# A transformer block on one core: the squares of x1 and the first down weights queued on VectorE and ScalarE behind the first product's second sum

## The chip, the core and the metric

The kernel runs on one core of a Trainium2 chip. A core has five engines that work side by side, each through its own queue in order: TensorE (PE; its weight loads are listed as PEld), VectorE (DVE), ScalarE (ACT), GpSimd (POOL) and SyncE (SP), which here issues all DMAs. The metric is the time of one execution in microseconds on the device. The kernel before takes 1398.54 us, the median of three runs from 1398.4 to 1398.91.

## The reference, cut to what matters

One layer of a hybrid block on 1024 tokens of width 1024, all in float32: a norm, a projection, three mixers (attention, a state-space scan, a gated recurrence), an output projection, and then the gated feed-forward part with 2816 inner columns that the change touches:

```
x = x + concatenate([att, ssd, lru]) @ w_out          # this is x1 below
h = rmsnorm(x, norm_ffn)                              # x1 * rsqrt(mean(x1^2)) * g
x = x + (silu(h @ w_gate) * (h @ w_up)) @ w_down
return rmsnorm(x, norm_final)
```

## The kernel before, in words

Everything is kept transposed, channels on the partitions and tokens along the row. Products in float32 are made from two halves: a high half (ACT copies the data in TensorE's rounded format) and a low half (DVE subtracts the high one from the source). Three matmuls, high by high, high by low and low by high, then stand for one. The helper `split` (L78 for ACT's copy, L69 for DVE's subtraction) does this, and `operand` makes such a pair in a tile of tag h.

`att_proj` ends the output projection. Each of its 16 units of 12 matmuls gives half a row block of x1; `finish` adds the residual (DVE, L75), scales it with the norm's weights (ACT), stores x1 to memory (`x1d`) and writes the pieces that the feed-forward products need, as split pairs, into tiles A and h.

The feed-forward products use a scheme with seven block products for eight. A product (`product(j, m, ...)`, j for one of 11 pairs of weight blocks, m = 0 for gate and 1 for up) loads a pair of weight blocks, wst and whi (l11, l12, l21, l22 are their halves), and makes four combinations of them in two tiles of tag t, s12 and s34. Seven chains of 12 matmuls follow (L955; the text calls them by the index of the pieces that they read): chains 0, 5, 6 and 4 add up in one bank x, and ACT copies its state after each of them (c11, c12, c21, c22); chains 1, 3 and 2 go to banks of their own (mm) and DVE and POOL add these to the copies. Chain 6 may start only when c12 has been copied out of x, chain 4 only after c21. For c21, POOL subtracts c21 from c12 (L69), and DVE then adds chain 3's bank to c21 (`add(V, c21, y2, c21)`, L1004). The four combinations are DVE's in the first product (0, 0) and POOL's in all others. In this text the first, second and third product are (0, 0), (0, 1) and (1, 0).

`squares` (L904) follows the first product in the program. It loads the eight row blocks of x1 again (L908; the first into ssum2, the other seven into tiles of tag g, which has two places), ACT squares each, and DVE adds seven of them to ssum2. `down_weights(0)` (L1013) loads a pair of w_down, makes four combinations of it on DVE in two tiles of tag t, and stores them. ssum2 is read by `rnorm_small` (L1072), 16 small matmuls behind the second product's chain 6; `factor` spreads its result over a tile r2 behind the third product's chain 5, and the gating of the first two pairs (`gated`, `to_down`) needs r2.

The order of the queues is set by a planner. It goes by its own clock through the program; among the instructions of an engine whose inputs are there and whose tiles have a place, it takes the one that stands first in the program. The engine then works in that order, whether or not the chip agrees with the planner's clock. A tag has a fixed number of places (wst 2, whi 2, t 4, g 2, e 4, h 16). `tc.issue_after(ins)` adds, for each instruction traced in its block that is on the same engine as `ins`, an edge that puts it behind `ins` on that engine's queue; instructions of other engines get none. `marks` lists matmuls: marks[1] is the last of the first product's chain 6.

Of the kernel before, what the change touches and what calls it, by code (L numbers as in the profile page):

```python
# [38 lines left out]
def tile_hybrid_block(ctx: ExitStack, tc: tile.TileContext, xT, w_in, w_dt, w_out, w_gu, w_dn, lru_g, prm,  # L39
                      c_ident, c_tri, c_last, c_alibi, outT, probe=None, stop=None):  # L40
    nc = tc.nc
    V, A, G, T = nc.vector, nc.scalar, nc.gpsimd, nc.tensor
# [16 lines left out]
    def bank():  # L59
        return psm.tile([P, H2], F32, name="mm", tag="mm")  # L60
# [7 lines left out]
    def sub(eng, out, a, b):  # L68
        return eng.tensor_tensor(out=out, in0=a, in1=b, op=ALU.subtract)  # L69
# [4 lines left out]
    def add(eng, out, a, b):  # L74
        return eng.tensor_tensor(out=out, in0=a, in1=b, op=ALU.add)  # L75

    def act(out, in_, func, **kw):
        return A.activation(out=out, in_=in_, func=func, **kw)  # L78
# [55 lines left out]
    def rnorm_small(sums, n, eps, pn_pool, tag="p1"):  # L134

        nb = sums[0].shape[-1] // P
        pn = pn_pool.tile([P, 8], F32, name=tag, tag=tag)[:, :nb]
        for tb in range(nb):
            for j, s in enumerate(sums):
                pn_last[0] = T.matmul(pn[:, tb:tb + 1], lhsT=s[:, tb * P:tb * P + P], rhs=ones[:, 0:1],  # L140
                                      start=(j == 0), stop=(j == len(sums) - 1))
        rn = sm.tile([P, 8], F32, name="rn", tag="rn")[:, :nb]
        rn_last[0] = rsqrt_small(rn, pn, n, eps)
        return rn
# [37 lines left out]
    with tc.tile_pool(name="np", bufs=2) as npool:  # L182
# [18 lines left out]
        last_mm = [None]  # L201
# [636 lines left out]
    def duo(pool, tag, dt=F32, bufs=None):  # L838
        return pool.tile([P, 2, H2], dt, name=tag, tag=tag, bufs=bufs)

    def combine_l(engs, s12, s34, l11, l12, l21, l22):
        e = iter(engs * 4)
        add(next(e), s12[:, 0], l21, l22)
        sub(next(e), s12[:, 1], s12[:, 0], l11)
        sub(next(e), s34[:, 0], l11, l21)
        sub(next(e), s34[:, 1], l12, s12[:, 1])
# [57 lines left out]
    def squares():  # L904

        for n in range(8):
            sq = ssum2 if n == 0 else slot(fp, "g", bufs=2)
            dma(out=sq, in_=x1d[n])  # L908
            act(sq, sq, AF.Square)
            if n:  # L910
                add(V, ssum2, ssum2, sq)

    NP = NFF // 2
    last_mm, last_hi = [None], [None]

    def operand(src):
        o = duo(hp, "h", F32R)
        act(o[:, 0], src, AF.Copy)
        sub(V, o[:, 1], src, f(o[:, 0]))
        return o  # L920

    def pair_loads(src, j):
        a, b = slot(wp, "wst", bufs=2), slot(wp, "whi", bufs=2)
        dma(out=a, in_=src[j])
        dma(out=b, in_=src[j + NP])
        return a, b
# [24 lines left out]
    def chain(ps, w, i, start, stop, ks=range(4)):  # L951
        for k in ks:
            ws = slice(k * P, k * P + P)
            for n, (wi, ai) in enumerate(((0, 0), (0, 1), (1, 0))):
                last_mm[0] = T.matmul(ps, lhsT=w[:, wi, ws], rhs=ops[k][i][:, ai], start=(start and k == 0 and n == 0),  # L955
                                      stop=(stop and k == 3 and n == 2), skip_group_check=not start)

    def product(j, m, ca, cb, hook=None):

        a, b = pair_loads(w_gu[m], j) if j or m else first[:2]  # L960
        l11, l12, l21, l22 = a[:, :H2], a[:, H2:], b[:, :H2], b[:, H2:]
        s12, s34 = duo(fp, "t", bufs=4), duo(fp, "t", bufs=4)
        if j or m:
            combine_l((G,), s12, s34, l11, l12, l21, l22)
        else:
            add(V, s12[:, 0], l21, l22)
            sub(V, s12[:, 1], s12[:, 0], l11)
            with tc.issue_after(last_put[0].ins):
                sub(V, s34[:, 0], l11, l21)
                sub(V, s34[:, 1], l12, s12[:, 1])  # L970
        x = psx.tile([P, H2], F32, name="x", tag="x")
        c11, c12, c21, c22 = ca[:, :H2], ca[:, H2:], cb[:, :H2], cb[:, H2:]
        if j == 0 and m == 0:

            y, y2, s2 = bank(), bank(), operand(s12[:, 1])
            chain(x, first[2][0], 0, True, True)
            chain(y, first[2][1], 1, True, True)
            for ks in (range(3), range(3, 4)):
                chain(y2, first[2][2], 3, True, True, ks)
                if ks[0] == 0:  # L980
                    act(c11, x, AF.Copy)
                chain(x, s2, 5, False, True, ks)
        else:
            chain(x, operand(l11), 0, True, True)
            y = bank()
            chain(y, operand(l12), 1, True, True)
            y2 = None
        if y2 is None:
            act(c11, x, AF.Copy)
        add(V, c11, y, c11)  # L990
        if y2 is None:
            chain(x, operand(s12[:, 1]), 5, False, True)
        marks.append(last_mm[0])
        if hook:
            hook()
        act(c12, x, AF.Copy)
        if y2 is None:
            y2 = bank()
            chain(y2, operand(l22), 3, True, True)
        chain(x, operand(s34[:, 0]), 6, False, True)  # L1000
        marks.append(last_mm[0])
        last_hi[0] = act(c21, x, AF.Copy)
        sub(G, c12, c12, c21)
        add(V, c21, y2, c21)  # L1004
        y = bank()
        chain(y, operand(s34[:, 1]), 2, True, True)
        chain(x, operand(s12[:, 0]), 4, False, True)
        marks.append(last_mm[0])
        act(c22, x, AF.Copy)
        add(G, c12, c12, c22)  # L1010
        add(V, c12, y, c12)

    def down_weights(j):  # L1013
        a, b = pair_loads(w_dn, j)
        s12, s34 = duo(fp, "t", bufs=4), duo(fp, "t", bufs=4)
        combine_l((V,), s12, s34, a[:, :H2], b[:, :H2], a[:, H2:], b[:, H2:])
        dma(out=wdd[0:2, j].rearrange("s p c -> p s c"), in_=s12)
        dma(out=wdd[2:4, j].rearrange("s p c -> p s c"), in_=s34)

    turn = [0]  # L1020
    marks = []

    def chunks():
        turn[0] += 1
        return [slot(fp, "g", bufs=2) if turn[0] % 3 == 0 else ev() for _ in range(2)]

    def gated(ga, gb):
        for g in (ga, gb):
            mul(V, g, g, r2[0])
            silu = act(g, g, AF.Silu)  # L1030
            mul(G, g, g, r2[0])
        return silu

    def to_down(j, ga, gb, ua, ub):
        mul(V, ga, ga, ua)
        mul(V, gb, gb, ub)
        t12, t34 = duo(wp, "wlo", bufs=2), duo(wp, "wlo", bufs=2)
        combine_r((V,), t12, t34, ga[:, :H2], ga[:, H2:], gb[:, :H2], gb[:, H2:])
        dma(out=sd[0, j], in_=ga[:, :H2])
        dma(out=sd[1:3, j].rearrange("s p c -> p s c"), in_=gb.rearrange("p (s c) -> p s c", s=2))  # L1040
        dma(out=sd[3:5, j].rearrange("s p c -> p s c"), in_=t12)
        dma(out=sd[5:7, j].rearrange("s p c -> p s c"), in_=t34)
# [13 lines left out]
    for j in range(NP):  # L1056
        ga, gb = chunks()
        product(j, 0, ga, gb, factor if j == 1 else None)
        if j == 0:
            with tc.issue_after(marks[1].ins):  # L1060
                squares()
                down_weights(j)
        else:
            silu = gated(ga, gb)
            if j == NP - 1:
                with tc.issue_after(silu.ins):
                    act(eps, ones[:, 0:1], AF.Sqrt)
            down_weights(j)
        ua, ub = chunks()
        product(j, 1, ua, ub)  # L1070
        if j == 0:
            with tc.issue_after(marks[4].ins):  # L1072
                late[0] = rnorm_small([ssum2], 1024.0, 1e-6, psy, tag="mm")
            held0 = ga, gb, ua, ub
        else:
            to_down(j, ga, gb, ua, ub)
# [226 lines left out]
```

## Time and profile before

| | us |
|---|---|
| median of 3 runs | 1398.54 |
| lowest, highest | 1398.4, 1398.91 |
| the profiled execution | 1396.86 |
| its span, first to last instruction | 1395.1 |

Times in the rows are microseconds from the start of the span; "mean ns" and forms are left as the profile prints them. "wst", "t" and so on are tile names with their numbers left out, so t<-whi is an instruction that reads tile whi and writes a tile t. In square brackets stands the engine's idle time before an instruction and what ended it. TensorE's granted clock is given as a share of 2.4 GHz; its other level is 1.2 GHz. SPq is the issue of a DMA, which lands later.

### The profile page before, as it was taken

The numbers are of one execution on the slowest core, as the hardware profiler recorded it, in microseconds if no ns is written. First come the engines' busy times: TensorE is split into PE (matmuls) and PEld (weight loads), VectorE is DVE, ScalarE is ACT, GpSimd is POOL, SyncE is SP. The second block draws the span as 40 slices with busy tenths as digits, with TensorE's granted clock in tenths as the row PEclk, the third lists the DMA queues.
The fourth block names the chain that finished last, engine by engine and source line by source line (L and its number), as shares of the span: only waits on it lengthen the run. The fifth ranks groups of instructions, "written<-read, shape, count | busy, mean of one in ns | idle before, by whom it ended". The sixth has DMA issues, their size and how long they took to land.

```text
span 1395.1 us, 18403 instructions
## 1 busy us (share of the span) xinstructions
PE 1341.3 (96%) x6786; PEld 1123.1 (81%) x6786; DVE 989.4 (71%) x1538; ACT 662.5 (47%) x1076; POOL 366.1 (26%) x265
## 2 busy tenths in 40 slices
PE   7999898999999899999979999999999999999996
PEld 6888588878888688788858878888888888888896
DVE  8667648988254677886797887876777676665655
ACT  5385746555232666765664433343332335543432
POOL 0022103766000000000005566664555642000000
PEclk9999999999999899999989999999999999999998
DMA  5112122332227865430356344444544348866523
GB/s 204 53 46 76 46 77 66 93 126 81 76 103 223 293 211 123 120 91 16 127 176 225 104 154 144 158 151 159 174 168 138 130 167 302 310 196 196 186 87 121
DMA packets 90266, 198.66 MB, mean 142 GB/s; under 512 B 9272, under 2 KB 23992, under 8 KB 90176
## 3 DMA queue, kind: packets, MB, share of 16 engines
q1 hardware_dynamic: 90176, 197.49, 43.0%
q8 instruction: 53, 0.87, 0.3%
q14 instruction: 37, 0.30, 0.1%
HBM read 142.64 MB, written 54.82 MB: 142 GB/s over the span
## 4 chain that ended last, share of the span: by engine, by line
PE 73%; DVE 11%; ACT 5%; DMA 5%; issue 3%; POOL 3%; SPq 0%; DVEq 0%; ACTq 0%; POOLq 0%
PE mm L98 17%; PE x L955 15%; PE mm L955 11%; PE mm L1106 11%; PE x L1106 4%; PE mm L425 2%; PE pt L726 2%; PE p L198 2%; DMA x1d<-e 1%; PE po L743 1%; PE sc L683 1%; PE sc L682 1%; DVE h L69 1%; PE po L745 1%; DMA acb<-acd 1%
## 5 line engine op out<-in xcount | busy, mean ns | idle before, releaser
L98 PE MATMUL mm<-h,whi 128*128 128x512 f32 x1184 | 373.4, 394 | 1.8 <-ACT h L78 1.1
L98 PEld LDWEIGHTS mm<-h,whi 128*128 128x128 f32 x1184 | 220.6, 188 | 46.6 <-ACT h L78 1.8
L98 PE MATMUL mm<-h,wlo 128*128 128x512 f32 x592 | 231.6, 392 | 0.0
L955 PE MATMUL x<-A,h 128*128 128x512 f32 x726 | 185.0, 398 | 4.5 <-ACT e L78 2.4
L955 PEld LDWEIGHTS x<-A,h 128*128 128x128 f32 x726 | 137.4, 190 | 37.4 <-ACT e L78 3.6
L75 POOL TENSOR_TENSOR t<-whi 128x512 f32<-128x512 f32 x21 | 32.7, 1557 | 458.3 <-DVE h L69 384.4
L1106 PE MATMUL mm<-h 128*128 128x512 f32 (+1 forms) x666 | 150.1, 378 | 0.0
L1106 PEld LDWEIGHTS mm<-h 128*128 128x128 f32 x666 | 120.2, 188 | 23.5 <-DVE h L69 0.4
L955 PE MATMUL mm<-A,h 128*128 128x512 f32 x528 | 136.4, 395 | 0.0
L98 PEld LDWEIGHTS mm<-h,wlo 128*128 128x128 f32 x592 | 111.5, 188 | 23.3 <-DVE wlo L69 0.3
L955 PEld LDWEIGHTS mm<-A,h 128*128 128x128 f32 x528 | 99.2, 188 | 23.1
L69 DVE TENSOR_TENSOR h<-t,h 128x512 fp32r<-128x512 f32 x97 | 100.4, 1052 | 20.6 <-ACT h L78 20.5
L78 ACT ACTIVATE e<-x 128x512 f32<-128x512 f32 x60 | 35.8, 596 | 129.1 <-PE x L955 114.1
L69 DVE TENSOR_TENSOR h<-wst,h 128x512 fp32r<-128x512 f32 (+1 forms) x70 | 77.4, 1124 | 24.5 <-ACT h L78 24.5
L955 PE MATMUL x<-h 128*128 128x512 f32 x330 | 92.4, 399 | 0.0
L955 PE MATMUL mm<-h 128*128 128x512 f32 x264 | 75.9, 398 | 8.2 <-ACT h L78 5.5
L78 ACT ACTIVATE whi<-wst 128x1024 fp32r<-128x1024 f32 x44 | 46.4, 1055 | 65.6 <-PE mm L98 52.1
L955 PEld LDWEIGHTS x<-h 128*128 128x128 f32 x330 | 63.4, 192 | 14.8
L78 ACT ACTIVATE h<-wst 128x512 fp32r<-128x512 f32 (+1 forms) x70 | 53.4, 786 | 36.6 <-DMA whi<-sd 11.6
L69 DVE TENSOR_TENSOR h<-whi,h 128x1024 fp32r<-128x1024 f32 (+1 forms) x47 | 53.5, 1138 | 23.9 <-ACT h L78 23.6
L69 DVE TENSOR_TENSOR wlo<-wst,whi 128x1024 fp32r<-128x1024 f32 x44 | 56.7, 1288 | 17.1 <-ACT whi L78 16.9
L955 PEld LDWEIGHTS mm<-h 128*128 128x128 f32 x264 | 49.8, 189 | 20.6 <-ACT h L78 5.9
(281 smaller groups left out, 2618.1 us busy)
## 6 DMA issues: line engine op xcount, KB each, us to landing
wst<-w_in SPq DMA_DIRECT2D x32, 512.0 KB, 3.6
qkl<-qkd SPq DMA_DIRECT2D x48, 256.0 KB, 5.7
wst<-w_gu SPq DMA_DIRECT2D x22, 512.0 KB, 4.4
whi<-w_gu SPq DMA_DIRECT2D x22, 512.0 KB, 5.4
wdd<-t SPq DMA_DIRECT2D x22, 512.0 KB, 4.7
sd<-wlo SPq DMA_DIRECT2D x22, 512.0 KB, 4.7
qkd<-e SPq DMA_DIRECT2D x16, 512.0 KB, 3.4
wst<-sd SPq DMA_DIRECT2D x28, 256.0 KB, 3.5
```

What stands on the lines that cost most here:

```text
L69: return eng.tensor_tensor(out=out, in0=a, in1=b, op=ALU.subtract)
L75: return eng.tensor_tensor(out=out, in0=a, in1=b, op=ALU.add)
L78: return A.activation(out=out, in_=in_, func=func, **kw)
L98: mm = T.matmul(ps, lhsT=w[:, ws], rhs=a[:, sl], start=(k == 0 and n == 0), stop=(k == nk - 1 and n == 2))
L198: last_mm[0] = T.matmul(os[hf], lhsT=w[:, ws], rhs=a[:, hf * H2:hf * H2 + H2], start=(kk == 0 and n == 0), stop=(kk == KD - 1 and n == 2))
L425: T.matmul(o, lhsT=a[k][:, ts], rhs=w, start=(k == 0 and n == 0), stop=(k == KD - 1 and n == 2))
L682: T.matmul(sc[:, :w], lhsT=qs[:, qc], rhs=ks[:, kc], start=True, stop=False)
L683: gate[0] = T.matmul(sc[:, :w], lhsT=qs[:, qc], rhs=kl[:, kc], start=False, stop=True)
L726: T.transpose(pt[:, j, qi * P:qi * P + P], pes[qi][:, kb * P:kb * P + P], ident)
L743: T.matmul(po[0:64, q0:], lhsT=va[:, 0:64], rhs=plo, start=False, stop=False)
L955: last_mm[0] = T.matmul(ps, lhsT=w[:, wi, ws], rhs=ops[k][i][:, ai], start=(start and k == 0 and n == 0), stop=(stop and k == 3 and n == 2 ...
L1106: mm = T.matmul(banks[n][:, cols], lhsT=w[:, 0, ws], rhs=a[:, 1, cols], start=(start and j == 0 and m == 0), stop=(stop and j == NP - 1 an ...
```

## The change

The block around `squares()` and `down_weights(0)` names two other instructions: DVE's add that completes c21 of the first product, and ACT's copy of c21. Both blocks are open at once, so what the two functions have on DVE stands behind the add, and what they have on ACT behind the copy. Their DMAs, on SP, get no edge.

```
-    last_mm, last_hi = [None], [None]
+    last_mm, last_hi, out_dve = [None], [None], [None]
...
         last_hi[0] = act(c21, x, AF.Copy)
         sub(G, c12, c12, c21)
-        add(V, c21, y2, c21)
+        out_dve[0] = add(V, c21, y2, c21)
...
         if j == 0:
-            with tc.issue_after(marks[1].ins):
+            with tc.issue_after(out_dve[0].ins), tc.issue_after(last_hi[0].ins):
                 squares()
                 down_weights(j)
```

## Rows read from the trace of the kernel before

**Rows 1.** The page's first part: busy time, share of the span, instructions.
```profile
PE 1341.3 (96%) x6786; PEld 1123.1 (81%) x6786; DVE 989.4 (71%) x1538; ACT 662.5 (47%) x1076; POOL 366.1 (26%) x265
```

**Rows 2.** Table of stretches: length, busy time (instructions) by engine, PEclk, DMA share, GB/s.
```profile
720.00:730.00 10.00, 1.85 (x4) 1.12 (x4) 7.70 (x12) 6.88 (x10) 0.00 (x0) 0.67 0.64 219
730.00:740.00 10.00, 7.93 (x25) 5.87 (x24) 10.00 (x15) 5.51 (x8) 3.09 (x1) 0.65 0.67 216
740.00:760.00 20.00, 20.00 (x89) 16.22 (x88) 15.63 (x17) 7.47 (x14) 15.64 (x10) 1.00 0.46 157
```

**Rows 3.** Timeline of TensorE: start, length, line, operation, tiles, count [idle time before].
```profile
719.47 0.61 PE L955 MATMUL mm<-h 128*128 128x512 f32 x2
725.55 0.79 PE L955 MATMUL mm<-h 128*128 128x512 f32 x1 [5.47 <-ACT h L78]
729.02 1.22 PE L955 MATMUL mm<-h 128*128 128x512 f32 x2 [2.68 <-DVE h L69]
...
733.17 3.36 PE L955 MATMUL x<-A,h 128*128 128x512 f32 x7 [2.07 <-DVE h L69]
...
737.31 1.54 PE L955 MATMUL mm<-A,h 128*128 128x512 f32 x6
```

**Rows 4.** Timeline of ACT, 716 to 747 us.
```profile
716.54 0.71 ACT L78 ACTIVATE t<-e,pr 128x512 f32<-128x512 f32 x1
721.31 1.06 ACT L78 ACTIVATE g<-g 128x1024 f32<-128x1024 f32 x1 [4.06 <-DMA g<-x1d]
...
744.51 0.63 ACT L78 ACTIVATE h<-t 128x512 fp32r<-128x512 f32 x1 [5.09 <-POOL t L69]
745.05 0.62 ACT L78 ACTIVATE h<-whi 128x512 fp32r<-128x512 f32 x1
...
746.09 0.58 ACT L78 ACTIVATE e<-x 128x512 f32<-128x512 f32 x1
```

**Rows 5.** Timeline of DVE, 700 to 751 us.
```profile
700.31 1.21 DVE L75 TENSOR_TENSOR ssum<-ssum,g 128x1024 f32<-128x1024 f32 x1
...
718.82 1.28 DVE L69 TENSOR_TENSOR t<-t 128x512 f32<-128x512 f32 x2
722.40 1.22 DVE L75 TENSOR_TENSOR ssum<-ssum,g 128x1024 f32<-128x1024 f32 x1 [2.30 <-ACT g L78]
...
730.09 1.21 DVE L75 TENSOR_TENSOR ssum<-ssum,g 128x1024 f32<-128x1024 f32 x1
...
732.43 0.68 DVE L69 TENSOR_TENSOR h<-t,h 128x512 fp32r<-128x512 f32 x1
733.03 0.68 DVE L75 TENSOR_TENSOR t<-wst,whi 128x512 f32<-128x512 f32 x1
...
739.52 1.28 DVE L69 TENSOR_TENSOR h<-wst,h 128x512 fp32r<-128x512 f32 x2
...
750.33 0.68 DVE L75 TENSOR_TENSOR e<-mm,e 128x512 f32<-128x512 f32 x1
```

**Rows 6.** Timeline of POOL, 736 to 770 us.
```profile
736.91 5.06 POOL L75 TENSOR_TENSOR t<-whi 128x512 f32<-128x512 f32 x1 [384.39 <-DVE h L69]
...
743.18 1.30 POOL L69 TENSOR_TENSOR t<-t,wst 128x512 f32<-128x512 f32 x1
...
746.75 1.41 POOL L69 TENSOR_TENSOR e<-e 128x512 f32<-128x512 f32 x1 [0.89 <-ACT e L78]
...
754.95 1.75 POOL L75 TENSOR_TENSOR e<-e 128x512 f32<-128x512 f32 x1
...
767.72 1.29 POOL L69 TENSOR_TENSOR t<-t,wst 128x512 f32<-128x512 f32 x1
```

**Rows 7.** All that line 908 issues: its loads of x1, issue to landing.
```profile
DMA to landing us min/median/max: 3.1/3.4/5.3
```

**Rows 8.** Timeline of TensorE: the statistics, and the next long wait.
```profile
762.28 1.84 PE L140 MATMUL mm<-ones,ssum 128*128 128x1 f32 x16
...
807.63 2.09 PE L955 MATMUL x<-A,h 128*128 128x512 f32 x6 [2.17 <-ACT e L78]
```

More of the change, by code (lines that the diff above doesn't have):

```diff
@@ L913, in tile_hybrid_block @@
     NP = NFF // 2
-    last_mm, last_hi = [None], [None]
+    last_mm, last_hi, out_dve = [None], [None], [None]
     def operand(src):
@@ L1003, in product @@
         sub(G, c12, c12, c21)
-        add(V, c21, y2, c21)
+        out_dve[0] = add(V, c21, y2, c21)
         y = bank()
@@ L1059, in tile_hybrid_block @@
         if j == 0:
-            with tc.issue_after(marks[1].ins):
+            with tc.issue_after(out_dve[0].ins), tc.issue_after(last_hi[0].ins):
                 squares()
```

## The prediction, made before the changed kernel was run

> **What bounds the kernel now.** The page comes first: TensorE is busy for 1341.3 of 1395.1 us [rows 1], so a change is worth what it takes from TensorE's remaining losses. The table of stretches shows the largest of them: from 720 to 740 us the granted clock averages 0.67 and 0.65, a mixture of 2.4 and 1.2 GHz, and 4 + 25 matmuls pass, against 89 in the next 20 us, 0.225 us apart [rows 2]. At that pace 29 matmuls are 6.5 us, so the place loses 13.5 us. TensorE's timeline gives its make-up: the engine runs dry at 720.08 (719.47 + 0.61), waits 5.47, 2.68 and 2.07 us, and goes on at full pace from 737.31 [rows 3]. The waits are 10.2 us; the other 3.3 are matmuls at half clock behind them. It waits for pieces of the first product's chains 3 and 5, each split into two halves, the high one by ACT, the low one by DVE.
>
> ACT's timeline names the cause: after the scaling of 716.54 it stands for 4.06 us before the Square of 721.31, whose load of x1 has not landed, and the splits queue behind that [rows 4]. DVE stands 2.30 us before the add of 722.40 that needs this Square [rows 5]. Neither is part of the product: both belong to the squares. Eight Squares, seven adds and the down weights' four combinations (from 733.03 on) stand among the product's pieces.
>
> **What the change removes.** These 19 instructions get edges behind c21's copy on ACT and c21's add on DVE. The old block named a matmul, and squares and down weights have no work on TensorE, so it held nothing. No other step changes in the code, but every queue is planned anew.
>
> Let E be the end of the first product's chain 5, now 737.31. DVE works without a gap up to 720.10 (718.82 + 1.28), and two adds like that of 700.31 stand in that work; without them it can be up to 2.4 us earlier, at 717.7. Of its instructions from 722.40 to 732.43, 12 remain when the three adds go, the last being the low half of chain 5's weights; with 0.60 from start to start (two in 1.28, one alone 0.68) they are 7.2 us [rows 5]. That half is then ready between 724.9 and 727.3, and the ten matmuls left of the chain take 2.3 us: E is 727.2 to 729.6 at full clock. Of the 3.3 us of slow matmuls I leave up to half, since some 3 us of waits remain in place of 10.2. The first gain is between 6.0 and 10.1 us; I take 9, near the upper end, since ACT's wait goes whole and the two early adds go for certain.
>
> **What takes its place.** Tag t has four places, and a product or a set of down weights takes two. The down weights' two are asked for ahead of the second product's, and are first written at 733.03, before POOL begins the second product at 736.91 [rows 5, 6]. I take it that the tiles of a tag are given out in the order of the program. ACT shows such a case for tag h: it idled 5.09 us and made l22's split at 745.05 only behind that of s12's second half at 744.51 [rows 4], though POOL had read the same whi since 736.91 [rows 6]. Then, after the change, POOL can begin the second product only when DVE, past c21's add, has reached the down weights' third combination.
>
> From E on: chain 2 covers c12's copy, chain 6 follows, 24 matmuls, E + 5.4. ACT copies c21 in 0.6, POOL subtracts in 1.4, DVE adds in 0.7 [rows 4 to 6], with 0.3 for passing on (an estimate from 746.09 + 0.58 to 746.75, three times): E + 8.4. Two squares' adds of 1.2 and two combinations of 0.60 stand ahead of the third: E + 12.0. POOL needs three combinations up to s12's second half. Undisturbed they take 1.29 each (767.72), 3.9 in all; now they take 7.6 (736.91 to 743.18 + 1.30) [rows 6]. ACT's split is 0.6, DVE's low half 0.7: the second product's chain 5 has its weights between E + 17.2 and E + 20.9, or 1.3 sooner if POOL makes that half second. Without them TensorE has chains 2, 6 and 4 of the first product and 0 and 1 of the second (chain 3 stands behind the same split on ACT): 60 matmuls, E + 13.5. It waits 2.4 to 7.4 us; I take 4.7, DVE being less crowded there than at 736.91, but not free. For the slow clock behind the wait I take 2.0, between the 3.3 above, after 10.2 us of waits, and nothing. So 6.7 us are given back, and E itself drops out: closing the first stall further makes the second no smaller.
>
> **What else moves.** The squares end later. They have two places of tag g, so a load waits for the add two before it: from add 3 (722.40) to add 5 (730.09) a round takes 7.7 us [rows 5]; at best it is a landing of 3.1 [rows 7], a Square of 1.06 and an add of 1.2, 5.4. Three rounds after add 1 are 16 to 23 us, so the sum is complete at E + 26 to E + 33. The statistics that read it, now at 762.28 [rows 8], come up on TensorE after four more chains, E + 13.5 + 6.7 + 10.8 = E + 31. I cost that at nothing, for the second wait hides it; with rounds of 7.7 us it is 2 us, and without that cover up to 9. On SP the loads and stores are the same; five loads of x1 move behind c21's add. The third product's pair is asked for when the down combinations have read their tiles, E + 13; its chain 0 comes some 18 us later, and x1's loads, of the same size, land within 5.3 [rows 7]. The wait of 2.17 at 807.63 [rows 8] hangs on ACT and DVE work behind the statistics, which come 2 us earlier with all else: nothing, bounded by the whole wait gained and 3 us lost. The moved Squares and adds themselves (8.5 and 8.4 us) fall under running chains.
>
> The sum is 9.0 - 4.7 - 2.0 = 2.3 us faster. The profiled execution took 1396.86 us (1.8 beside its span), which gives 1394.6; the median of the runs, 1398.54, is 1.7 above it and gives 1396.2.
>
> **Rivals.** *The gain is kept.* If a tile goes to whoever is ready, POOL starts the second product when its pair lands, and no second wait opens. For it: no row shows two ready requests of tag t at odds. Against it: the split of 745.05. Then the statistics stand at E + 24.3, at least 1.7 us before their sum, so it gives 9 less 1.7, 1391.2.
>
> *POOL is shut out while DVE catches up.* The combination of 736.91 took 5.06 us against 1.29 for that of 767.72 [rows 6], while DVE worked without a gap until 740.80 (739.52 + 1.28) [rows 5]; after the change POOL falls into the stretch in which DVE works off the queued adds and combinations. With the three at 7.6 us and c22's addition (1.75 at 754.95 [rows 6]) ahead of s12's second half, the wait is 7.4 + 1.75, with 3.3 for the clock 12.5: 3.5 us slower, 1402.0. Against it: the squares' adds come singly, each behind a load. It decides the sign when the three together take more than some 5 us with c22's addition ahead of them, 6.5 without. The Trainium skill, page "SBUF — State Buffer", section "Who interferes with whom", says that VectorE with two SBUF inputs and a GpSimd instruction that reads SBUF share a read interface as an exclusive lock: the later one waits for the whole other instruction. By strict turns the three would take 3 x (1.29 + 0.60) = 5.7 us, an estimate, and the change would gain 1.5 us, 1397.0; the 5.06 of the row is longer than any turn, so the trace agrees that one blocks the other and not that they alternate.
>
> *Nothing much moves.* If the plan fills the freed places of ACT and DVE with other pieces that wait for loads, the first stall remains: 1398.5. Against it: the 4.06 us on ACT had only the squares' load in front.
>
> **Chances.** The forecast (both waits, 1391.5 to 1400) 0.50; the gain kept 0.16; POOL shut out 0.20; nothing moves 0.14. A measurement of this kernel can tell 0.2%, 2.8 us, from no change. The forecast lies beyond it in 0.22, within in 0.26, slower in 0.02; the gain kept is all faster; POOL shut out is slower in 0.15, within in 0.05; nothing moves divides into 0.02, 0.10 and 0.02. Together: faster 0.40, the same 0.41, slower 0.19. A range that leaves out 2 in 10 reaches from a little below the kept gain to the slower rival, 1390 to 1402.
>
> **What would show it.** Right: no Square before c21's copy on ACT; chain 5 of the first product ending before 731; POOL's first t<-whi just behind the third down combination on DVE; a new wait of TensorE before the second product's chain 5, released by ACT's or DVE's split of a tile t. Wrong: POOL's t<-whi ahead of the down combinations, a wait of more than 3 us before the statistics, or the stall of 720 still there.

## The result, and the profile after

The changed kernel takes 1410.30 us, the median of four runs from 1408.81 to 1412.04, beside 1398.72 (1398.40 to 1399.33) for the kernel before in the same runs: a ratio of 1.0094, 95% interval 1.0078 to 1.0109. It is slower by some 12 us, where 2.3 us faster was forecast; it lies above the range of 1390 to 1402.

The profiled execution took 1408.81 us with a span of 1407.0, 11.9 more than before. The work is the same; the page's first part answers to [rows 1].

```profile
PE 1346.2 (96%) x6786; PEld 1124.9 (80%) x6786; DVE 990.6 (70%) x1538; ACT 661.6 (47%) x1076; POOL 367.6 (26%) x265
```

The tables of stretches, columns as in [rows 2], the kernel after and then the kernel before over the same four stretches from 712 to 830 us:

```profile
720.00:730.00 10.00, 9.06 (x28) 6.73 (x29) 5.89 (x10) 3.38 (x6) 0.00 (x0) 0.68 0.30 105
730.00:740.00 10.00, 10.00 (x45) 8.16 (x44) 3.56 (x4) 3.92 (x5) 4.89 (x4) 1.00 0.01 2
740.00:760.00 20.00, 15.58 (x59) 11.57 (x59) 16.89 (x18) 8.07 (x13) 9.06 (x6) 0.91 0.76 263
...
712.00:735.00 23.00, 19.92 (x74) 15.09 (x73) 13.49 (x23) 8.61 (x16) 0.00 (x0) 0.85 0.27 102
735.00:762.00 27.00, 22.58 (x90) 17.27 (x89) 22.41 (x22) 13.43 (x21) 15.95 (x10) 0.94 0.56 195
762.00:800.00 38.00, 33.41 (x150) 26.87 (x149) 31.07 (x36) 16.71 (x25) 24.63 (x15) 0.91 0.40 138
800.00:830.00 30.00, 24.15 (x96) 18.59 (x95) 23.23 (x22) 9.30 (x15) 19.15 (x11) 0.94 0.44 149
```

```profile
712.00:735.00 23.00, 12.78 (x44) 9.13 (x44) 20.70 (x32) 14.30 (x23) 0.00 (x0) 0.75 0.60 201
735.00:762.00 27.00, 27.00 (x114) 21.91 (x113) 22.08 (x26) 10.29 (x18) 18.73 (x10) 0.96 0.55 179
762.00:800.00 38.00, 37.45 (x179) 30.80 (x179) 28.62 (x35) 15.88 (x25) 22.54 (x14) 1.00 0.36 133
800.00:830.00 30.00, 27.83 (x114) 22.21 (x113) 23.66 (x23) 10.30 (x17) 20.85 (x12) 0.94 0.47 149
```

Count the matmuls. From 712 to 735 the changed kernel passes 30 more; from 735 on it passes 24, 29 and 18 fewer. Its first product began 2.8 us earlier (709.44 against 712.28, the first row of line 955 in each timeline), so that 12 of its matmuls lie before 712. This lead is outside the change: it is there already at the last row of line 682, before the projection (649.4 against 652.2), and the first products of all the traces here begin between 708.5 and 713.9. Of line 955's matmuls, 382 lie between 700 and 830 us, against 413 before: 31 fewer, 7.1 us at 0.23 us each. With the lead of 2.8 us, 9.9 us are lost between the start of the first product and 830. Up to 1150 it is 47 fewer (1748 against 1795), another 3.7 us; they go around four small waits between 992 and 1113, 2.7 us of idle time together. The rest, some 1 us, is lost after line 955.

TensorE's timeline shows where; it answers to [rows 3, 8].

```profile
718.00 0.49 PE L955 MATMUL mm<-h 128*128 128x512 f32 x1 [0.81 <-ACT h L78]
719.84 1.22 PE L955 MATMUL mm<-h 128*128 128x512 f32 x2 [1.34 <-DVE h L69]
...
722.85 3.35 PE L955 MATMUL x<-A,h 128*128 128x512 f32 x7 [0.94 <-DVE h L69]
...
726.87 1.56 PE L955 MATMUL mm<-A,h 128*128 128x512 f32 x6
...
741.78 0.73 PE L955 MATMUL x<-A,h 128*128 128x512 f32 x2 [0.87 <-ACT h L78]
...
744.01 0.73 PE L955 MATMUL mm<-A,h 128*128 128x512 f32 x2 [0.97 <-ACT h L78]
747.32 2.93 PE L955 MATMUL x<-A,h 128*128 128x512 f32 x6 [2.58 <-DVE h L69]
...
767.23 1.16 PE L955 MATMUL x<-A,h 128*128 128x512 f32 x2 [3.05 <-ACT h L78]
769.94 4.21 PE L955 MATMUL x<-A,h 128*128 128x512 f32 x9 [1.55 <-ACT g L78]
...
779.84 1.84 PE L140 MATMUL mm<-ones,ssum 128*128 128x1 f32 x16
781.55 2.32 PE L955 MATMUL mm<-A,h 128*128 128x512 f32 x9
...
804.69 4.11 PE L955 MATMUL x<-A,h 128*128 128x512 f32 x15 [1.16 <-DVE h L69]
...
818.24 1.85 PE L955 MATMUL mm<-A,h 128*128 128x512 f32 x4 [4.58 <-DVE h L69]
```

The first stall fell from 10.2 to 3.1 us idle, and three others came: 4.4 us before the second product's chains 5 and 3 (741 to 747), 4.6 at 767 to 770 (3.05 before the fourth product's chain 0, 1.55 before the third's chain 5), and 5.7 in place of 2.2 near 804 to 818. Matmuls at 1.2 GHz stand behind the waits: the granted clock averages 0.91 from 762 to 800, where it was 1.00. The row of 781.55 is the third product's chain 1. In every trace of this case it comes only behind the statistics; before the change it stood at 769.60. So from 764 to 780 TensorE has only chains of bank x to run.

POOL's timeline answers to [rows 6]:

```profile
735.11 1.29 POOL L69 TENSOR_TENSOR e<-e 128x512 f32<-128x512 f32 x1 [383.13 <-ACT e L78]
736.36 1.30 POOL L75 TENSOR_TENSOR t<-whi 128x512 f32<-128x512 f32 x1
...
739.33 1.73 POOL L69 TENSOR_TENSOR t<-t,wst 128x512 f32<-128x512 f32 x1
...
755.80 1.29 POOL L75 TENSOR_TENSOR t<-whi 128x512 f32<-128x512 f32 x1 [10.83 <-DMA whi<-w_gu]
```

c21's subtraction now stands first, and the second product's combinations behind it, though that product's pair was asked for before 723. Then POOL waits 10.83 us for the third product's pair. DVE's timeline answers to [rows 5]:

```profile
736.44 0.69 DVE L75 TENSOR_TENSOR e<-mm,e 128x512 f32<-128x512 f32 x1 [7.38 <-POOL e L69]
737.05 1.17 DVE L75 TENSOR_TENSOR t<-wst,whi 128x512 f32<-128x512 f32 x1
...
744.36 1.70 DVE L75 TENSOR_TENSOR ssum<-ssum,g 128x1024 f32<-128x1024 f32 x1
745.98 0.68 DVE L69 TENSOR_TENSOR t<-whi,t 128x512 f32<-128x512 f32 x1
746.58 0.68 DVE L69 TENSOR_TENSOR h<-t,h 128x512 fp32r<-128x512 f32 x1
...
759.26 1.78 DVE L69 TENSOR_TENSOR t<-t,wst 128x512 f32<-128x512 f32 x1
...
768.04 1.21 DVE L75 TENSOR_TENSOR ssum<-ssum,g 128x1024 f32<-128x1024 f32 x1
...
773.75 1.70 DVE L75 TENSOR_TENSOR ssum<-ssum,g 128x1024 f32<-128x1024 f32 x1
...
814.77 1.75 DVE L69 TENSOR_TENSOR wlo<-e,wlo 128x512 f32<-128x512 f32 x1
816.44 1.75 DVE L69 TENSOR_TENSOR h<-whi,h 128x512 fp32r<-128x512 f32 x1
```

DVE stood idle for 7.38 us while the first product's chains ran, and then had the queued work on its hands: an add and a combination stand ahead of the split of 746.58 that TensorE waited for. The last add ends at 775.45. ACT's timeline, answering to [rows 4], shows the Squares behind c21's copy, and two waits that did not exist before:

```profile
734.44 0.60 ACT L78 ACTIVATE e<-x 128x512 f32<-128x512 f32 x1 [5.70 <-PE x L955]
734.93 1.05 ACT L78 ACTIVATE ssum<-ssum 128x1024 f32<-128x1024 f32 x1
...
766.55 0.63 ACT L78 ACTIVATE h<-wst 128x512 fp32r<-128x512 f32 x1 [0.98 <-DMA wst<-w_gu]
769.29 0.60 ACT L78 ACTIVATE g<-x 128x512 f32<-128x512 f32 x1 [2.11 <-DVE ssum L75]
```

g<-x is the third product's c11, in a place of tag g that a square held until DVE's add of 768.04 had read it. Until this copy is done the third product's chain 5 can't add to its bank x. The split of 766.55 is the fourth product's, for its chain 0 in the other bank x. Its load went out only when DVE's combination of 759.26 had read the second down weights (759.26 + 1.78 = 761.04):

```profile
761.49 0.46 SPq L924 DMA_DIRECT2D wst<-w_gu  x1
```

The loads of the second down weights, in turn, go out from 744.86 on, after the second product's combinations, which stand behind c21's subtraction, have read their pair. The loads of line 908 that come after 735 land in 5.5 us (median), those of [rows 7] in 3.4:

```profile
DMA to landing us min/median/max: 3.2/5.5/6.8
```

### The profile page after: what moved, and what is told of

Read it like the earlier page. It is cut to its first block, busy times and chain, and to the rows that moved or that the text cites. A ratio compares the mean times of both kernels' runs of the same rounds, so it can differ in the third digit from the quotient of the medians.

```text
span 1407.0 us, 18399 instructions
## 1 busy us (share of the span) xinstructions
PE 1346.2 (96%) x6786; PEld 1124.9 (80%) x6786; DVE 990.6 (70%) x1538; ACT 661.6 (47%) x1076; POOL 367.6 (26%) x265
## 4 chain that ended last, share of the span: by engine, by line
PE 53%; DVE 14%; POOL 11%; issue 9%; DMA 8%; ACT 5%; SPq 0%; DVEq 0%; POOLq 0%; ACTq 0%
PE mm L98 17%; PE mm L1106 11%; POOL t L69 4%; PE x L1106 4%; PE x L955 3%; DMA whi<-w_gu 3%; DVE h L69 2%; PE mm L425 2%; PE pt L726 2%; PE mm L955 2%; DVE wlo L69 2%; PE p L198 2%; DMA whi<-w_dn 2%; POOL t L75 1%; PE po L743 1%
## 5 line engine op out<-in xcount | busy, mean ns | idle before, releaser
L955 PE MATMUL x<-A,h 128*128 128x512 f32 x726 | 191.5, 406 | 13.1 <-DVE h L69 7.3
L1106 PEld LDWEIGHTS mm<-h 128*128 128x128 f32 x666 | 120.3, 188 | 23.5 <-DVE h L69 0.3
L69 POOL TENSOR_TENSOR e<-e 128x512 f32<-128x512 f32 x15 | 20.4, 1359 | 391.8 <-ACT e L78 391.8
L69 DVE TENSOR_TENSOR h<-t,h 128x512 fp32r<-128x512 f32 x97 | 96.3, 1014 | 7.7 <-ACT h L78 7.4
L75 DVE TENSOR_TENSOR e<-mm,e 128x512 f32<-128x512 f32 x45 | 30.7, 683 | 60.2 <-POOL e L69 50.7
L69 DVE TENSOR_TENSOR h<-whi,h 128x1024 fp32r<-128x1024 f32 (+1 forms) x47 | 49.6, 1055 | 25.0 <-ACT h L78 25.0
```

Source lines behind the costliest of these rows:

```text
L1106: mm = T.matmul(banks[n][:, cols], lhsT=w[:, 0, ws], rhs=a[:, 1, cols], start=(start and j == 0 and m == 0), stop=(stop and j == NP - 1 an ...
```

## The experiments

Each ratio is to the kernel before on the same chip. "Held" means behind c21's copy on ACT and c21's add on DVE. All start from the changed kernel; the block is the one that the diff touches. wlo is a tag whose two places stand empty from the projection's end to the first gating. Each edit makes the planner order all queues anew, so a ratio holds the new plan as well as the part that the edit names. The kernels with one square leave out the other seven and so compute another norm; only their time is used.

| edit | median us | ratio, 95% interval |
|---|---|---|
| squares alone held | 1400.39 | 1.0019, 1.0006 to 1.0031 |
| down weights alone held | 1405.68 | 1.0058, 1.0042 to 1.0075 |
| both held by the edge on DVE alone | 1406.60 | 1.0069, 1.0052 to 1.0086 |
| both held, squares in wlo (two places) | 1411.82 | 1.0103, 1.0086 to 1.0120 |
| both held, squares in four places | 1403.58 | 1.0044, 1.0026 to 1.0061 |
| squares alone held, four places | 1392.48 | 0.9965, 0.9951 to 0.9980 |
| the same, edge on ACT alone | 1393.66 | 0.9972, 0.9961 to 0.9983 |
| nothing held, four places | 1397.15 | 1.0002, 0.9991 to 1.0014 |
| squares 3 to 7 held, four places | 1395.09 | 0.9973, 0.9960 to 0.9987 |
| the same and down weights held | 1405.40 | 1.0045, 1.0028 to 1.0061 |
| both held, down sums in wlo | 1409.89 | 1.0081, 1.0057 to 1.0104 |
| one square, down weights held | 1398.11 | 1.0002, 0.9990 to 1.0014 |
| one square, down weights free | 1389.10 | 0.9947, 0.9930 to 0.9964 |
| one square, down weights held in wlo | 1391.15 | 0.9964, 0.9947 to 0.9980 |

**Each part alone.**

```
+            with tc.issue_after(out_dve[0].ins), tc.issue_after(last_hi[0].ins):
+                squares()
+            down_weights(j)
```

> Only the squares stand behind c21's copy and add; the down weights' combinations are free again, as before the change. Theory S (the squares): their late chain, eight Squares and seven adds through two places of tag g, holds the place that the third product's c11 needs (TensorE idle 3.05 + 1.55 us at 764 to 770 in the changed kernel) and makes the statistics 17.6 us late, which leaves DVE behind at 813.7 (4.58 us idle). By it this kernel keeps most of the loss: 1405 to 1411 us. Rival D (the down weights): their combinations behind c21's add make the third product's pair late (POOL stands 10.8 us for it until 755.8) and the stalls come from there. By it this kernel has the gain of the first stall and no loss: 1387 to 1394 us.

```
+            squares()
+            with tc.issue_after(out_dve[0].ins), tc.issue_after(last_hi[0].ins):
+                down_weights(j)
```

> Only the down weights' combinations stand behind c21's add; the squares are free again. Theory S: the stall of some 10 us idle at 720 is back, since ACT again stands in front of a Square whose load has not landed, and the stalls at 764 and 813 are gone: 1396 to 1401 us, not to be told from the kernel before. Rival D: the first stall is partly back and the loss of the late down weights stays: 1404 to 1412 us.

Neither theory has it alone. The down weights by themselves cost 0.58%, within D's range; the squares by themselves 0.19%, which is less than S asked for and more than D allowed. With the squares held and the down weights free, POOL does the second product's combinations when their load lands (timelines of POOL, of ACT and of TensorE in that kernel):

```profile
725.26 2.60 POOL L75 TENSOR_TENSOR t<-whi 128x512 f32<-128x512 f32 x1 [373.82 <-DMA whi<-w_gu]
```

```profile
759.59 1.06 ACT L78 ACTIVATE g<-g 128x1024 f32<-128x1024 f32 x1 [2.81 <-DMA g<-x1d]
```

```profile
761.70 0.74 PE L955 MATMUL x<-A,h 128*128 128x512 f32 x2 [2.87 <-ACT h L78]
```

The first stall is as short as in the changed kernel, but ACT now stands before late Squares (4.10, 3.51 and 2.81 us, the last at 759.59), and TensorE behind it: what made the stall of 720 [rows 3, 4] has moved 40 us on. With the down weights held and the squares free, the first stall is back (9.4 us idle) and a new one is there as well (POOL, then TensorE):

```profile
743.67 1.30 POOL L69 TENSOR_TENSOR e<-e 128x512 f32<-128x512 f32 x1 [392.65 <-ACT e L78]
744.92 1.29 POOL L75 TENSOR_TENSOR t<-whi 128x512 f32<-128x512 f32 x1
```

```profile
750.31 0.74 PE L955 MATMUL x<-A,h 128*128 128x512 f32 x2 [2.04 <-ACT h L78]
...
753.56 3.35 PE L955 MATMUL x<-A,h 128*128 128x512 f32 x7 [2.00 <-DVE h L69]
```

**One edge alone.** In the block, `with tc.issue_after(out_dve[0].ins):` around both calls.

> The edge on DVE alone, for squares and down weights, two places of g as in the changed kernel; the Squares on ACT are free. The adds behind c21's add hold the two places, so only Squares 0 to 2 can run early. Theory T: the down weights' lateness is that of the changed kernel: TensorE waits again near 741 to 747 and near 764, 1402 to 1411 us. Rival (the edge on ACT is the harmful one): 1395 to 1400 us.

T's numbers, in the time and in the trace: waits of 1.37 and 3.14 us end at 741.60 and 746.00, one of 4.16 at 767.74. The edge on ACT is not the harmful one.

**The squares' places.** First two other places, then four:

```
-            sq = ssum2 if n == 0 else slot(fp, "g", bufs=2)
+            sq = ssum2 if n == 0 else slot(wp, "wlo", bufs=2)
```

> The changed kernel, with the squares' seven tiles in the two places of tag wlo, which stand empty from the projection's end to the first gating, in place of the two of tag g. Everything else of the change stays. Theory S: the third product's c11 and c21 no longer wait for the squares' adds, so the 1.55 us in front of g<-x at 768 go and part of the 3.05 us before them; the statistics stay late and with them the stall of some 4.6 us at 813. In all 3 to 6 us less than the changed kernel: 1404 to 1407 us. Rival D: no difference from the changed kernel, 1409 to 1412 us. If the holding of the g tiles is the whole of the loss (a stronger form of S), 1396 to 1400 us.

```
+            sq = ssum2 if n == 0 else slot(*((fp, "g"), (fp, "g"), (wp, "wlo"), (wp, "wlo"))[(n - 1) % 4], bufs=2)
```

> The changed kernel, both edges kept for the squares and the down weights, with the squares in four places (two of g, two of wlo). It closes a table of two by two with the changed kernel (held down weights, two places), the squares alone held (free down weights, two places: 1.0019 of before) and the squares alone held in four places (0.9965). If the two losses add up, held down weights cost about 0.9% beside either: 1403 to 1408 us. If the squares' waits for their loads were the larger part and the down weights only cover the rest, 1396 to 1401 us.

> The squares alone behind c21's copy and add, as in the first experiment, but in four places, two of g and two of wlo. Theory A: the loads of squares 1 to 4 land while ACT still waits for c21, and the 2.81 us that ACT stood before a Square at 759 shrink, and with them TensorE's 2.87 us there: 2 to 5 us less than with two places, 1395 to 1399 us. Rival (the late sum, not the loads, decides): no less than with two places, 1400 to 1402 us.

Two places of wlo gain nothing, which is D's number and not S's: TensorE's wait for a copy g<-x shrinks from 1.55 to 0.22 us, but the last add still comes late (780.14) and TensorE waits 2.58 us before 776.29 and 4.90 before 819.09. Holding g is not the loss by itself. Four places gain 0.50% with the down weights held (1.0094 to 1.0044) and 0.54% with them free (1.0019 to 0.9965), and held down weights cost 0.75 and 0.79%: the two losses add. (The squares alone in four places gained more than A had asked for.) The changed kernel against "four places, squares alone held" is 1.3%, both together. That last kernel is faster than the changed kernel and the kernel before; its chains run from 735 to 762 without a wait, where the squares alone held in two places passed 102 matmuls:

```profile
735.00:762.00 27.00, 27.00 (x119) 21.90 (x118) 20.76 (x26) 16.89 (x25) 12.49 (x7) 1.00 0.65 211
```

Is the edge needed, then, and which one? With four places, the edge on ACT alone, and no edge at all:

```
+            with tc.issue_after(last_hi[0].ins):
+                squares()
+            down_weights(j)
```

> The squares in four places, held by the edge on ACT alone (c21's copy); no edge on DVE, the down weights free. The adds follow their Squares in any case. Theory A (the Squares' place on ACT, and the loads they wait for, are what counts): the same as with both edges on the squares, 1391 to 1395 us. Rival (the edge on DVE keeps the adds from the product's pieces and gives part of the gain): 1395 to 1399 us.

```
+            squares()
+            down_weights(j)
```

> No edge at all, for squares or down weights: the kernel before, with the squares in four places instead of two. Theory A: the load of the fourth square no longer waits for a place, so the 4.06 us that ACT stood at 721 go for the most part, and with them 5 to 8 us of TensorE's first stall, without any edge: 1390 to 1395 us. Rival (the Squares' and adds' own time among the product's pieces, 8.5 and 8.4 us, makes the first stall, whether they wait or not): 1396 to 1400 us.

With four places the edge on ACT is all that is needed. Without it, four places change nothing in the time, which is the rival's number: the first stall is 8.0 us idle in place of 10.2, 5.60 of it in one wait, and ACT stands before the fourth square although its place is free (ACT, then the queue of DMAs):

```profile
720.59 1.06 ACT L78 ACTIVATE wlo<-wlo 128x1024 f32<-128x1024 f32 x1 [2.91 <-DMA wlo<-x1d]
```

```profile
710.95 3.33 SPq L898 DMA_DIRECT2D x1d<-e x2
717.35 0.80 SPq L908 DMA_DIRECT2D wlo<-x1d x2
```

The last two of x1's row blocks are stored at 710.95 and after. The first of these stores takes 6.3 us to land (717.25), the load that reads it back goes out at 717.35 and lands 3.2 us later, and the Square starts at 720.59, whatever place it has. The store, and not a place, made ACT's wait at 720. How much of TensorE's first stall is this wait, and how much the Squares' and adds' own time, as the rival has it, no run separates: the edge takes both away.

**Squares 0 to 2 free, 3 to 7 held.** `squares(range(3))` ahead of the block, `squares(range(3, 8))` in it, four places; first with the edge on ACT alone and free down weights, then with both edges around the squares and the down weights.

> Squares 0 to 2, whose loads land during the projection, are free as before the change; squares 3 to 7 stand behind c21's copy on ACT alone; the squares' tiles alternate between the two places of g and the two empty ones of wlo; the down weights are free. Theory A (ACT stands before a Square whose load has not landed, wherever that Square is put: 4.06 us at 721 before the change, 2.81 us at 759 with the squares alone held): with four places and five Squares the loads have landed when their turn comes, no Square is waited for, the stall of 720 is as small as in the changed kernel and none takes its place: 1388 to 1395 us. Rival P (the new plan of the queues behind 830, not the Squares' loads, costs what the squares alone held lost): 1397 to 1401 us.

> As the split of the squares (0 to 2 free, 3 to 7 behind, four places), but the squares 3 to 7 and the down weights' combinations stand behind c21's copy and c21's add. Theory T (the held down weights take two places of tag t ahead of the second product, so that POOL's combinations of the second product come behind c21's subtraction and everything after them is late): 5 to 10 us more than the split with free down weights, whatever that is. Rival: the loss with held down weights came from their meeting with eight late squares; then no more than 3 us.

The first lies just above A's range, and its first stall is 4.8 us idle, not the 3.1 of the changed kernel. The held down weights add 0.72%, 10 us, the most that T expected. Holding all the squares is as good as holding five.

**What held down weights cost.** The second product needs two places of tag t, and so do the held sums. Put these in wlo, and nothing else changes:

```
-        s12, s34 = duo(fp, "t", bufs=4), duo(fp, "t", bufs=4)
+        s12, s34 = (duo(wp, "wlo", bufs=2) if j == 0 else duo(fp, "t", bufs=4) for _ in range(2))
```

> The changed kernel with the first down weights' combinations in the two empty places of tag wlo in place of two of tag t; both edges stay, for the squares and for the down weights. Theory T: POOL begins the second product's combinations when its pair lands, near 725 to 728, ahead of c21's subtraction; the waits of 741 to 747 go, and the time falls to that of the squares alone held: 1398 to 1402 us. Rival (the late reading of the down weights' pair holds the places of wst and whi, whatever the tag of the sums): the stall of 764 stays, 1404 to 1410 us.

T's mechanism was there and its time was not; the time is the rival's. POOL begins at 726.73, and behind the first stall TensorE has no wait of half a microsecond up to 757, but then one of 6.19 us, behind a Square that ACT waited 5.14 us for. This wait hangs on a Square's load and not on a late pair of weights, so the chains had only come sooner to the other loss (ACT, TensorE):

```profile
761.82 1.06 ACT L78 ACTIVATE g<-g 128x1024 f32<-128x1024 f32 x1 [5.14 <-DMA g<-x1d]
```

```profile
763.41 4.21 PE L955 MATMUL x<-A,h 128*128 128x512 f32 x9 [6.19 <-ACT e L78]
```

So the same again with that loss taken out, `for n in range(1)` in `squares`: down weights held, free, and held with their sums in wlo.

> The changed kernel with only the first of the eight squares: seven loads of x1, seven Squares and seven adds are left out (the norm is then that of one row block alone). Theory S: no stall at 764 and none at 813, the statistics as early as before or earlier: 1388 to 1396 us, below the kernel before since the stall at 720 is gone too. Rival D: the waits at 741 to 747 and the third product's late pair stay: 1401 to 1408 us. Rival C (POOL and DVE in each other's way, no matter which of the moved instructions): part of the loss goes with the adds, 1397 to 1402 us.

> Only the first of the eight squares is computed (the other seven loads, Squares and adds are left out, as in the earlier kernel with one square, which took 1.0002 of before with held down weights), and the down weights are free. With so few squares there is nothing left for ACT to wait for. If held down weights cost 0.75 to 0.8% by themselves, as in the table of two by two: 1385 to 1389 us. If they cost only what meets the squares: 1394 to 1398 us.

> Only the first square again (the other seven left out); the down weights held behind c21's add, but their four combinations in the two empty places of wlo instead of two of tag t. Theory T (the two places of tag t, which put POOL's combinations of the second product behind c21's subtraction, are the whole cost of the held down weights): the same as with free down weights, 1385 to 1389 us. Rival (their late reading, which keeps places of wst and whi and so the third product's pair, is the larger part): 1393 to 1398 us.

With one square and held sums the time fell into C's range, above S's and below D's, and the next kernel says why: held costs 0.55% here (1.0002 against 0.9947), less than the 0.75 to 0.8 of the table of two by two. The sums in wlo in place of t take back 0.38 of these 0.55, between what T and its rival asked for. In all kernels with sums held in t, POOL's first t<-whi stands right behind c21's subtraction; in the other experiments it comes at 725 to 733, ahead of it. The rest of 0.17% is within the intervals; the profile of the kernel with held sums in wlo has 4.8 us of waits at 792 to 800, which the free one lacks.

## Why the prediction was wrong

**The first stall: right.** Chain 5 ended at 726.87, against 737.31; less the earlier start of 2.8 it is a gain of 7.6, within 6.0 to 10.1 and below the 9 taken. The idle time alone fell by 7.1, so of the 3.3 us of slow matmuls only 0.5 came back, where I had counted on at least half: the granted clock still averages 0.68 from 720 to 730.

**The second wait: its size right, its place wrong.** It was to be 4.7 us idle and is 4.4, before the chains named. But I had POOL wait for the down weights' third combination (742.07); it began at 736.36, ahead of even the first (737.05). The order of tag t is real, as sums in wlo show, yet it acts in the plan, which sets POOL's queue: c21's subtraction first, the combinations behind it. No tile is waited for on the chip. Of the wait, 2.58 us hang on a split of DVE behind an add and a combination, which I had not counted. So that the size fits is partly luck: POOL began 2.5 us sooner than the forecast's E + 12, and DVE lost about as much. With the slow clock the second wait cost 6.6 us, against 6.7 forecast: the second product and the third's chain 0 are done at 764.18 (763.32 + 0.86), against 769.76 before, of which the statistics, then ahead of them, are 1.7. That is a lead of 3.9 us, 2.8 of it the earlier start. Up to there the change gains 1.0 us where the sum has 2.3.

**"What else moves", costed at nothing: the step that failed.** The terms put at nothing cost 10.9 us from there to 830 (a gain of 1.0 had become a loss of 9.9), and 3.7 more behind 990. With E at 726.87 they were to be: sum complete at E + 33 at the latest, measured E + 48.6 (775.45); statistics at E + 31, measured E + 53 (779.84); the third product's pair asked for at E + 13, measured E + 17.4 and E + 20.3, with POOL able to start on it at E + 28.9 (755.80). A round of the squares was taken at 5.4 to 7.7 us; the three from 739.84 to 773.75 took 11.3 each. Pushed behind one point, four of the five late loads of x1, the down weights' stores and two pairs of weights meet in 740 to 760, at 263 GB/s where 720 to 740 had 219 and 216 [rows 2], and land later; and the Squares and adds wait among the second product's pieces.

Three things meet at 767 to 770. The third product's c11 needs a place of g that a square holds: the prediction knew of the two places, and asked only who of the squares waits for them. The fourth product's pair comes late, two pairs behind the held down weights. And chain 1, which could have filled the gap, stands behind the late statistics. The prediction looked for the cost of a late sum in a wait at the statistics; no such wait came. That the late work costs the time is shown by the table of two by two: four places for the squares give back 0.5%, 7 us, and free down weights 0.75%, 10 us; either is about what the first stall returned. How each of the two is shared among these three waits is read from the trace and was not tested one by one.

**The wait at 807: bounded too closely.** It was to lose 3 us at most and lost 3.6 in idle time. The gating of two pairs, let loose together by the later r2, stands ahead of the split of 816.44 on DVE. What decides whether this wait appears stays open: it is absent with all squares held and down weights free, and there with one square and held down weights (1.91 and 2.74 us), but also with squares 3 to 7 held and down weights free (2.37 and 1.21).

**The rivals.** The slower rival came nearest in time, for a reason that the trace denies: POOL was not shut out, its three combinations took 4.7 us (736.36 to 739.33 + 1.73), near the undisturbed 3.9. The chance of slower was 0.19, and 0.15 of it rested on that one mechanism; the late squares, costed at "without that cover up to 9", had none. Of the marks set for "wrong", POOL's t<-whi ahead of the down weights' combinations came true.

The small waits of 0.4 to 0.9 us from 992 to 1113, one every 40 us, have no counterpart in the kernel before. Faster and slower kernels among the experiments have such waits, of 0.3 to 1.4 us (the squares alone held in four places from 977 to 1097, the squares in wlo from 1033 to 1114); why is open, and no run was made for them.

## What to carry to other kernels

An instruction that waits for a load stops everything behind it on its engine's queue (4.06 us on ACT, [rows 4]); moving it back helps only if its data and its place have come by then, so move it together with enough places for its loads, and check who else wants these. Hold back only the work that does the harm: here the Squares on ACT, not the weights' sums that stood beside them in the block, for work held back also holds its tiles, and its sources with them, and the products behind it wait (moving the tiles alone gave back 0.38 of 0.55%; the sources' share is read from the trace). When a step is costed at "hidden", work out its end with the transfers that the same move pushes together.

## What the runs showed of the hardware

With both engines busy, DVE's adds of 128x1024 took 1.70 and 2.30 us in place of 1.21, and POOL's 128x512 operations 1.7 to 2.2 in place of 1.29. The Trainium skill, page "SBUF — State Buffer", section "SBUF: two separate sides", says that of a VectorE instruction with two SBUF inputs and a GpSimd instruction that reads SBUF, the one that starts first holds the shared ports for the whole instruction and the other waits. The trace agrees for most single instructions: 2.30 is 1.21 and most of one of POOL's 1.29. Over a row of both, DVE goes on at about half its pace (756.95 to 764.90, 7.9 us for what takes 3.5 alone) and POOL at three quarters.

It does not agree where one operation of POOL met a row of DVE's that was already under way without a gap: POOL then waited for the end of the row and not of one instruction. In five traces such an operation took 4.35 to 6.21 us and ended 1.15 to 1.17 us after the row's last instruction, while DVE kept its pace. The 5.06 of [rows 6] is one: it ends at 741.97, DVE's row at 740.80. In each case it was one operation of POOL, and no row of them, as the rival had it.
